# A two-layer hybrid encoder on one core: softmax rows divided after the weighted sum, with the inverse row sums turned on TensorE and spread through DRAM

## The chip, the cores and the metric

The kernel runs on one core of one Trainium2 chip. The metric is the device time of one execution in microseconds (us). Three runs of the kernel before gave a median of 2450.9 us (2449.78 to 2452.65); one further execution was profiled.

## The reference

Two layers, each of them a half-step SwiGLU feed-forward, a mixer with three branches, and a second half-step feed-forward, on 512 tokens of 1024 channels in f32. The change lies in the two attention branches of the mixer, A (chunked, with a learned bias by distance) and C (causal, with cumulative forget gates as bias); each has 8 heads of 64 channels. For one head:

```python
qf = rms_norm(q, gq) * (dh ** -0.5)
kf = rms_norm(k, gk)
logits = einsum('bqhd,bkhd->bhqk', qf, kf) + bias      # masked entries: -1e30
p = softmax(logits, axis=-1)
out = einsum('bhqk,bkhd->bqhd', p, v)
```

The outputs of all heads are concatenated, multiplied by a branch matrix, gated, summed over the branches and multiplied by an output matrix.

## The kernel before

**Arithmetic.** Nearly every product of f32 matrices is made of three TensorE matmuls: each operand is split into a high part (a cast, on ScalarE) and a low part (source minus high part, mostly on VectorE); `triple` (lines 119 to 121) issues high x high, high x low and low x high. `wchunk` loads a 512 KB piece of weights and splits it (cast on line 271, subtraction on line 273). `split_to` does the same for activations (lines 378 and 379).

**Order of the work.** Python code emits the instructions. A counter `pe[0]` adds up nominal TensorE work (one unit is about one 512-column matmul). `later(delay, fn)` puts a step into a list with a due time on that counter, and `poll()`, called before every `triple`, runs what has come due. The tile framework then places each emitted instruction in its engine's queue, and may move it ahead of others. Every engine works through its queue in order.

**Attention.** `attention` goes through the 8 heads, and in a head through 4 blocks of 128 queries (`logits(h, i)`, with (i+1) x 128 keys). Between the blocks a *filler* emits other TensorE work: for branch A the projections of branch C (`fill_a`), for branch C the merge of branch A's output (`fill_c`). One block does this:

1. `logits`: two matmuls into a PSUM tile `mm` (lines 951, 952); VectorE adds the bias, negates and takes the row minimum (line 955, `mx`); ScalarE takes the exponential and, in the same instruction, the row sums `sm` (line 959); VectorE inverts them (`rs`, line 961); the exponentials are multiplied by `rs`, on GpSimd for blocks 0 to 2 and on VectorE for block 3 (line 962).
2. `turn`, 24 units later: TensorE transposes the 128x128 pieces (line 974), ScalarE casts the result (line 978), VectorE subtracts (line 979).
3. `weigh`, 14 units after every second block: TensorE multiplies with the values (lines 996, 997). The two halves of the output stand in two halves of the partitions; ScalarE copies one (line 1000), VectorE adds the other (line 1001), and `split_to` makes the high part on ScalarE and the low part on GpSimd (line 379), 64 partitions by 256 queries each.

Two heads make a *pair* p: their outputs are the lower and the upper 64 partitions of one output tile. PSUM has four tiles `mm` and four tiles `acc`; SBUF has 17 tiles of the tag `b` (4 KB a partition), which hold queries, keys, outputs and weights in turn, two of `t1` and three of `t2`.

**Queries and keys.** `proj_qk` projects, sums squares by head, computes the inverse norms and multiplies the four tiles by them (line 839, two on VectorE and two on GpSimd). Its inner `turn(p)` transposes a pair and writes the scaled result: on ScalarE to a head's own partitions (line 853), and for queries a second time, on ScalarE, to the other 64 partitions (line 856); the low part is made on VectorE (line 859).

**Other GpSimd work at that time.** Memsets for the low parts (line 857), the causal mask added to the bias strips of branch C (`strip_c`, line 937). DMAs are issued by SyncE's queue, except the four per layer that save x to DRAM (line 1119, GpSimd's queue).

Of the kernel before, what the change touches and what calls it, by code (L numbers as in the profile page):

```python
# [15 lines left out]
F32 = mybir.dt.float32  # L16
F32R = mybir.dt.float32r
I32 = mybir.dt.int32
AF = mybir.ActivationFunctionType
ALU = mybir.AluOpType  # L20
AX = mybir.AxisListType

P = 128
T = 512
# [6 lines left out]
HD = 64  # L31
NT = T // P
# [8 lines left out]
def encoder_kernel(tc, xT, c, w_ada, b_ada, gains, w_gate, w_up, w_down, w_qkv, w_f, w_ubg,  # L41
# [22 lines left out]
    def st(shape, dt, tag, bufs):  # L64
        return sb.tile(shape, dt, tag=tag, bufs=bufs, name=nm(tag))
# [4 lines left out]
    def mmt(shape=(P, T)):  # L70
        return ps.tile(list(shape), F32, tag="mm", bufs=4, name=nm("mm"))

    def blk(tag, dt=F32R):
        bufs = {"xv": 4, "v2": 4, "b": NB}[tag]
        return st([P, 2, T], dt, tag, bufs)
# [22 lines left out]
    def later(delay, fn, group=None):  # L98
        t = Task(pe[0] + delay, fn, group)
        tasks.append(t)  # L100
        return t
# [70 lines left out]

    x_dram = dr.tile([4, P, 2 * T], F32, name="x_dram")
    fv_dram = [dr.tile([H, FVLEN], F32, name=f"fv_dram{l}") for l in range(L)]

    last = {}

# [199 lines left out]
    def split_to(hi, lo, src, lo_eng=nc.vector):  # L377
        nc.scalar.copy(hi, src)  # L378
        lo_eng.tensor_tensor(lo, src, hi.bitcast(F32), op=ALU.subtract)  # L379
# [438 lines left out]
    def proj_qk(l, col, gcol, is_q, res, pre=None, norm=None):  # L818
        lows = []
        qs = []  # L820

        def evac(t, a):
            if t == 0:
                qs.extend((st([P, NT, T], F32, "ptb", 2), st([P, NT, H], F32, "qss", 1)))
            qn, ss = qs
            nc.scalar.copy(qn[:, t, :], a)
            sq = t2(T)
            nc.scalar.activation(sq, a, AF.Square)  # L828
            nc.vector.tensor_reduce(ss[:, t, :], sq.rearrange("p (h d) -> p h d", h=H), axis=AX.X, op=ALU.add)

        yield from proj(l, col, evac, pre, norm)
        qn, ss = qs
        v = st([P, NT * H], F32, "nt_v32", 2)
        nc.vector.tensor_scalar(v, ss.rearrange("p t h -> p (t h)"), 1.0 / HD, EPS, op0=ALU.mult, op1=ALU.add)
        r = rsqrt(v, NT * H)
        for t in range(NT):
            q3 = qn[:, t, :].rearrange("p (h d) -> p h d", h=H)
            eng = nc.vector if t % 2 else nc.gpsimd
            eng.tensor_tensor(q3, q3, r[:, t * H:(t + 1) * H].unsqueeze(2).to_broadcast([P, H, HD]), op=ALU.mult)

        def turn(p):
            pt = mmt()
            for t in range(NT):
                nc.tensor.transpose(pt[:, t * P:(t + 1) * P], qn[:, t, p * P:(p + 1) * P], ident)
            pe[0] += 2.2
            b = blk("b")
            if is_q:
                lows.append(blk("b"))
            first, second = slice(0, HD), slice(HD, P)
            for odd, (own, other) in enumerate(((first, second), (second, first))):  # L850
                dst = b[:, odd, :]
                gc = gcol[own, :]
                nc.scalar.activation(dst[own, :], pt[own, :], AF.Identity, scale=gc)
                low = dst[other, :]
                if is_q:
                    nc.scalar.activation(low, pt[own, :], AF.Identity, scale=gc)
                    nc.gpsimd.memset(lows[p][other, odd, :].bitcast(F32), 0.0)
                    low = lows[p][own, odd, :]
                nc.vector.scalar_tensor_tensor(low, pt[own, :], gc, dst[own, :].bitcast(F32),
                                               op0=ALU.mult, op1=ALU.subtract)  # L860
            res.append((b, lows[p]) if is_q else b)

        todo = [lambda p=p: turn(p) for p in range(4)]
        turns.append(todo)

        def ready(p):
            if len(todo) >= 4 - p:
                if heads[0] < (Q_GATE if is_q else K_GATE)[p]:
                    later(8, lambda: ready(p))
                else:  # L870
                    while len(todo) >= 4 - p:
                        todo.pop(0)()

        for p in range(4):
            later(TURN + 12 * p, lambda p=p: ready(p))
# [64 lines left out]
    def attention(qs, ks, vs, strip, ys, filler, budget, group):  # L940


        open_pt = {}

        def logits(h, i, strips):
            p, off = divmod(h, 2)
            (q, ql), k = qs[p], ks[p]
            odd = h % 2
            n = (i + 1) * P
            s = mmt()  # L950
            mm(s[:, :n], q[:, odd, i * P:(i + 1) * P], k[:, odd, :n], start=True, stop=False)
            mm(s[:, :n], ql[:, odd, i * P:(i + 1) * P], k[:, odd, :n], start=False, stop=True)
            lg = t1(T)[:, :n]
            mx = st([P, 1], F32, "mx", 4)
            nc.vector.tensor_tensor_reduce(out=lg, in0=s[:, :n], in1=strips[i], scale=-1.0, scalar=BIG,
                                           op0=ALU.add, op1=ALU.min, accum_out=mx)
            pr = t2(T)[:, :n]
            sm = st([P, 1], F32, "sm", 4)
            nc.scalar.activation(pr, lg, AF.Exp, bias=mx, scale=-1.0, accum_out=sm)
            rs = st([P, 1], F32, "rs", 4)  # L960
            nc.vector.reciprocal(rs, sm)
            (nc.vector if i == NT - 1 else nc.gpsimd).tensor_scalar(pr, pr, rs, None, op0=ALU.mult)
            pe[0] += 0.5 * (i + 1.5)
            later(LAG_T, lambda: turn(h, i, pr), group)

# [18 lines left out]
        def weigh(h, half, pt):  # L984
            p, off = divmod(h, 2)
            rows = slice(off * HD, off * HD + HD)
            other = slice(HD - off * HD, 2 * HD - off * HD)
            if off == 0 and half == 0:
                ys.append(blk("b"))
            y = ys[p]  # L990
            o = mmt((P, HALF))
            nj = 2 * half + 2
            for j in range(nj):
                q0 = P if j == nj - 1 else 0
                v2 = vs[j][:, h, :, :].rearrange("p a d -> p (a d)")
                mm(o[:, q0:], v2, pt[:, 0, j, q0:], start=(j == 0), stop=False)  # L996
                mm(o[:, q0:], v2, pt[:, 1, j, q0:], start=False, stop=(j == nj - 1))  # L997
            cols = slice(half * HALF, (half + 1) * HALF)
            yl = t1(T)[:, :HALF]
            nc.scalar.copy(yl[rows, :], o[other, :])  # L1000
            nc.vector.tensor_tensor(yl[rows, :], o[rows, :], yl[rows, :], op=ALU.add)
            split_to(y[rows, 0, cols], y[rows, 1, cols], yl[rows, :], nc.gpsimd)
            pe[0] += 1.0 * nj

        for h in range(H):
            strips = strip(h)
# [13 lines left out]
            for _ in filler:  # L1020
                pass

    LAG_T, LAG_V = 24, 14


    def pool_front(l, g):
# [244 lines left out]
```

## Time and profile before

| what | before |
|---|---|
| median of three runs | 2450.9 us |
| profiled execution | 2450.88 us |
| its span, first to last instruction | 2448.9 us |
| mean granted TensorE clock | 0.998 |
| instructions | 34028 |

The span leaves 2.0 us of the profiled execution outside. In the profile PE is TensorE's matmuls and PEld its weight loads (each matmul has one, which overlaps the matmul ahead of it), DVE is VectorE, ACT ScalarE, POOL GpSimd, SP SyncE. A name such as L974 is the line of the kernel. "mm<-ident,t" says that an instruction writes a tile `mm` and reads `ident` and a tile of tag `t1` or `t2` (numbers in names are left out). An idle stretch of an engine is put down to the instruction that ended it, its releaser.

### The profile page before, as it was taken

To read this page: it belongs to the slowest core of one execution; us is meant where nothing else is said; L and a number is where in the kernel's file an instruction comes from. 1 tells how busy PE (TensorE), PEld (TensorE's weight loads), DVE (VectorE), ACT (ScalarE), POOL (GpSimd) and SP (SyncE) were. 2 spreads that over 40 slices of the span, in tenths; PEclk is the share of its full clock that TensorE was granted. 3 is DMA by queue.
4 is the path that set the end of the run, shared out by engine and by line. 5 is a ranking of instruction groups with operands and counts; after the bars stand their busy time and mean duration, and the time that the engine had idled before them with its cause. 6 is when DMAs were issued, how large, how long until landed. Compare 5 with 4: busy or idle time off the path is not lost. (4 is left out here: it accounts for less than half of the span.)

```text
span 2448.9 us, 34028 instructions
## 1 busy us (share of the span) xinstructions
PE 2396.8 (98%) x12966; PEld 2051.8 (84%) x12966; DVE 1600.5 (65%) x2859; ACT 1110.3 (45%) x1888; POOL 377.3 (15%) x439
## 2 busy tenths in 40 slices
PE   7999999999999999999999999999999999999999
PEld 5798888777888898988898888878777888988888
DVE  8978766677643378787678656477765434765463
ACT  5333345677642353333453334366765333533341
POOL 3000002144532110000000000123354322000000
PEclk9999999999999999999999999999999999999999
DMA  7756543222323426565327423223133234233232
GB/s 284 251 170 209 198 147 113 78 82 88 116 91 103 142 75 240 174 206 198 129 85 243 138 86 121 103 90 96 61 109 99 95 111 139 87 104 112 67 114 78
DMA packets 116279, 320.23 MB, mean 131 GB/s; under 512 B 11122, under 2 KB 13298, under 8 KB 116116
## 3 DMA queue, kind: packets, MB, share of 16 engines
q1 hardware_dynamic: 114962, 313.86, 38.3%
q0 software_dynamic: 1152, 4.19, 0.4%
q8 instruction: 102, 1.67, 0.3%
q14 instruction: 61, 0.50, 0.1%
q10 hardware_dynamic: 2, 0.00, 0.0%
HBM read 311.64 MB, written 6.38 MB: 130 GB/s over the span
## 5 line engine op out<-in xcount | busy, mean ns | idle before, releaser
L271 ACT CAST whi<-raw 128x1024 fp32r<-128x1024 f32 (+1 forms) x325 | 338.2, 1044 | 595.1 <-PE mm L120 289.2
L273 DVE TENSOR_TENSOR wlo<-raw,whi 128x1024 fp32r<-128x1024 f32 x317 | 392.2, 1240 | 197.4 <-ACT whi L271 194.2
L121 PE MATMUL mm<-hhi,wlo 128*128 128x512 f32 x744 | 289.8, 390 | 0.7 <-DVE wlo L273 0.4
L119 PE MATMUL mm<-hhi,whi 128*128 128x512 f32 x744 | 290.2, 390 | 0.0
L120 PE MATMUL mm<-hlo,whi 128*128 128x512 f32 x744 | 290.0, 390 | 0.0
L119 PE MATMUL acc<-b,whi 128*128 128x512 f32 (+1 forms) x704 | 264.1, 376 | 1.7 <-ACT b L378 1.7
L121 PE MATMUL acc<-b,wlo 128*128 128x512 f32 (+1 forms) x704 | 262.1, 374 | 3.5 <-DVE wlo L273 3.5
L120 PE MATMUL acc<-b,whi 128*128 128x512 f32 (+1 forms) x704 | 262.4, 373 | 0.0
L197 DVE CUSTOM_DVE_ANT_0 v<-v,b,badac 128x1024 f32<-128x1024 f32 x144 | 188.3, 1316 | 60.9 <-DMA v<-in_w_ada_dram 60.7
L119 PE MATMUL acc<-hhi,whi 128*128 128x512 f32 x480 | 190.7, 399 | 1.7 <-ACT hhi L738 1.7
L121 PE MATMUL acc<-hhi,wlo 128*128 128x512 f32 x480 | 188.9, 394 | 0.0
L120 PE MATMUL acc<-hlo,whi 128*128 128x512 f32 x480 | 188.5, 393 | 0.2 <-DVE hlo L741 0.2
L121 PEld LDWEIGHTS mm<-hhi,wlo 128*128 128x128 f32 x744 | 139.7, 188 | 30.9 <-DVE wlo L273 1.6
L119 PEld LDWEIGHTS mm<-hhi,whi 128*128 128x128 f32 x744 | 140.0, 188 | 27.9
L120 PEld LDWEIGHTS mm<-hlo,whi 128*128 128x128 f32 x744 | 139.7, 188 | 27.4
L121 PEld LDWEIGHTS acc<-b,wlo 128*128 128x128 f32 x704 | 133.8, 190 | 27.2 <-DVE wlo L273 4.6
L119 PEld LDWEIGHTS acc<-b,whi 128*128 128x128 f32 x704 | 133.3, 190 | 23.8 <-ACT b L378 2.6
L120 PEld LDWEIGHTS acc<-b,whi 128*128 128x128 f32 x704 | 133.3, 189 | 23.2 <-DVE b L379 0.9
L119 PE MATMUL acc<-whi,hhi 128*128 128x512 f32 x336 | 137.7, 411 | 4.4 <-ACT t L828 3.7
L120 PE MATMUL mm<-b,whi 128*128 128x512 f32 (+1 forms) x384 | 135.8, 354 | 0.0
L119 PE MATMUL mm<-b,whi 128*128 128x512 f32 (+1 forms) x384 | 135.8, 354 | 0.0
L121 PE MATMUL mm<-b,wlo 128*128 128x512 f32 (+1 forms) x384 | 135.6, 354 | 0.0
(300 smaller groups left out, 5598.3 us busy)
## 6 DMA issues: line engine op xcount, KB each, us to landing
v<-in_w_ada_dram SPq DMA_DIRECT2D x144, 512.0 KB, 4.4
raw<-in_w_down_dram SPq DMA_DIRECT2D x88, 512.0 KB, 3.5
raw<-in_w_up_dram SPq DMA_DIRECT2D x82, 512.0 KB, 3.4
b<-in_w_gate_dram SPq DMA_DIRECT2D x76, 512.0 KB, 5.3
raw<-in_w_ubg_dram SPq DMA_DIRECT2D x56, 512.0 KB, 3.3
raw<-in_w_qkv_dram SPq DMA_DIRECT2D x42, 512.0 KB, 3.7
raw<-in_w_branch_dram SPq DMA_DIRECT2D x24, 512.0 KB, 3.6
raw<-in_w_out_dram SPq DMA_DIRECT2D x16, 512.0 KB, 3.3
```

The costliest lines, as they stand in the source:

```text
L119: mm(o, lh, rh, start=start, stop=False, skip_group_check=onto)
L120: mm(o, lh, rl, start=False, stop=False, skip_group_check=onto)
L121: mm(o, ll, rh, start=False, stop=stop, skip_group_check=onto)
L197: dot = nc.vector.tensor_tensor_reduce(out=raw, in0=raw, in1=silc[0], scale=1.0, scalar=badac[:, l, j, d:d + 1], op0=ALU.mult, op1=ALU.add ...
L271: nc.scalar.copy(hi, raw)
L273: lo_eng.tensor_tensor(lo, raw, hi.bitcast(F32), op=ALU.subtract)
```

## The change

In words:

- **The division moves.** The exponentials are transposed and multiplied with the values undivided. The eight row sums of a pair (two heads, four blocks) are collected in the columns of one 128x8 tile. 26 units after the pair's last exponential, `send` inverts it on VectorE, turns it on TensorE into 8x128, copies it out of PSUM on ScalarE and writes it to DRAM (4 KB, GpSimd's queue). 24 units later `spread` reads it back twice (GpSimd's queue), 512 inverse sums broadcast over the 64 partitions of each head. 20 units later `norm_rows` multiplies the pair's whole output by it (VectorE, 128x512) and splits it: cast on ScalarE, subtraction on VectorE.
- `weigh` now leaves its f32 sum in a tile of tag `b` (output and inverse sums of the pair), and no longer splits it.
- **Norms.** All four tiles of line 839 are multiplied on VectorE.
- **Second query copies.** GpSimd copies them from the first ones in SBUF, where ScalarE wrote them from PSUM.

```diff
+    inv_dram = {(g, p): dr.tile([2 * NT, P], F32, name=f"inv_dram_{g}{p}") for g in "ac" for p in range(4)}
...
-            eng = nc.vector if t % 2 else nc.gpsimd
+            eng = nc.vector
...
                 if is_q:
-                    nc.scalar.activation(low, pt[own, :], AF.Identity, scale=gc)
+                    nc.gpsimd.tensor_copy(low, dst[own, :])
...
+        sums, rows_of = {}, {}
...
-            sm = st([P, 1], F32, "sm", 4)
-            nc.scalar.activation(pr, lg, AF.Exp, bias=mx, scale=-1.0, accum_out=sm)
-            rs = st([P, 1], F32, "rs", 4)
-            nc.vector.reciprocal(rs, sm)
-            (nc.vector if i == NT - 1 else nc.gpsimd).tensor_scalar(pr, pr, rs, None, op0=ALU.mult)
+            if odd == 0 and i == 0:
+                sums[p] = st([P, 2 * NT], F32, "sm", 2)
+            nc.scalar.activation(pr, lg, AF.Exp, bias=mx, scale=-1.0,
+                                 accum_out=sums[p][:, odd * NT + i:odd * NT + i + 1])
+            if odd and i == NT - 1:
+                later(LAG_S, lambda: send(p), group)
...
             if off == 0 and half == 0:
-                ys.append(blk("b"))
-            y = ys[p]
+                rows_of[p] = st([P, 2, T], F32, "b", NB)
+            y = rows_of[p][:, 0, :]
...
-            nc.vector.tensor_tensor(yl[rows, :], o[rows, :], yl[rows, :], op=ALU.add)
-            split_to(y[rows, 0, cols], y[rows, 1, cols], yl[rows, :], nc.gpsimd)
+            nc.vector.tensor_tensor(y[rows, cols], o[rows, :], yl[rows, :], op=ALU.add)
             pe[0] += 1.0 * nj
+
+        def send(p):
+            rs = st([P, 2 * NT], F32, "rs", 1)
+            nc.vector.reciprocal(rs, sums[p])
+            tp = mmt()
+            nc.tensor.transpose(tp[:2 * NT, :P], rs, ident)
+            flat = st([2 * NT, P], F32, "flat", 1)
+            nc.scalar.copy(flat, tp[:2 * NT, :P])
+            pe[0] += 0.5
+            nc.gpsimd.dma_start(inv_dram[group, p], flat)
+            later(LAG_R, lambda: spread(p), group)
+
+        def spread(p):
+            for off in range(2):
+                r = inv_dram[group, p].rearrange("(h i) q -> h (i q)", h=2)[off:off + 1, :]
+                nc.gpsimd.dma_start(rows_of[p][off * HD:(off + 1) * HD, 1, :], r.broadcast_to([HD, T]))
+            later(LAG_N, lambda: norm_rows(p), group)
+
+        def norm_rows(p):
+            y = blk("b")
+            ys.append(y)
+            full = rows_of[p][:, 0, :]
+            nc.vector.tensor_tensor(full, full, rows_of[p][:, 1, :], op=ALU.mult)
+            split_to(y[:, 0, :], y[:, 1, :], full)
...
-    LAG_T, LAG_V = 24, 14
+    LAG_T, LAG_V, LAG_S, LAG_R, LAG_N = 24, 14, 26, 24, 20
```

Behind the first added line all line numbers rise, so that line 955 of before is line 957 of the changed kernel, 979 is 982, 1001 is 1004, 273 is 274 and 937 is 938.

The queues show the move at three places, all in branch C of the first layer. VectorE before, for one head (`t` and `lg` are tiles of `t1` and `t2`; `rs` are the inverse sums of one block, `mx` its row minimum):

```order
L961 RECIPROCAL rs_6113<-sm_6111 128x1
L979 TENSOR_TENSOR ptb_6044<-mm_6119,ptb_6044 128x4x128
L955 ISA t_1255_6135,mx_6136<-mm_6132,strip_6051 128x384
L955 ISA mx_6136 128x1
L979 TENSOR_TENSOR pta_6144<-mm_6145,pta_6144 128x128
L961 RECIPROCAL rs_6141<-sm_6139 128x1
L1001 TENSOR_TENSOR t_1263_6164<-mm_6155,t_1263_6164 64x256
L955 ISA t_1266_6180,mx_6181<-mm_6177,ssum_6053 128x512
```

VectorE in the changed kernel, from the inverse sums of a pair (line 1009) on:

```order
L1009 RECIPROCAL rs_5669<-sm_5312 128x8
L274 TENSOR_TENSOR wlo_5793<-raw_5790,whi_5792 128x1024
L1004 TENSOR_TENSOR b_5474<-mm_5630,t_1090_5635 64x256
L957 ISA t_1099_5661,mx_5662<-mm_5658,strip_5610 128x256
L957 ISA mx_5662 128x1
L982 TENSOR_TENSOR ptb_5603<-mm_5676,ptb_5603 128x4x128
```

And seven rows on, around the multiplication of that pair's output (line 1028):

```order
L982 TENSOR_TENSOR pta_5697<-mm_5720,pta_5697 128x2x128
L957 ISA t_1116_5733,mx_5734<-mm_5730,ssum_5612 128x512
L957 ISA mx_5734 128x1
L1028 TENSOR_TENSOR b_5474<-b_5474 128x512
L274 TENSOR_TENSOR wlo_5929<-raw_5926,whi_5928 128x1024
```

The reciprocal that stood behind every block's row minimum is gone; one for eight blocks stands in its place, and 13 rows behind it the multiplication, which waits for both reads of `spread`; behind it stand the next weights' low parts (line 274).

GpSimd before, for about one head (line 962 multiplies a block by its inverse sums, line 379 makes a low part, line 937 adds the mask to a bias strip):

```order
L962 TENSOR_SCALAR t_1146_5755<-t_1146_5755,rs_5758 128x128
L379 TENSOR_TENSOR b_5589<-t_1150_5769,b_5589 64x256
L962 TENSOR_SCALAR t_1161_5800<-t_1161_5800,rs_5803 128x256
L962 TENSOR_SCALAR t_1168_5828<-t_1168_5828,rs_5831 128x384
L379 TENSOR_TENSOR b_5589<-t_1174_5854,b_5589 64x256
L937 TENSOR_TENSOR strip_6051<-strip_6051,cmask 128x128 x3
L937 TENSOR_TENSOR ssum_5900<-ssum_5900,cmask 128x128
```

GpSimd in the changed kernel, for one pair of heads:

```order
L938 TENSOR_TENSOR strip_5766<-strip_5766,cmask 128x128 x3
L938 TENSOR_TENSOR ssum_5612<-ssum_5612,cmask 128x128
L1015 DMA inv_dram_c_127<-flat_5673 8x128
L1021 DMA b_5474<-inv_dram_c_127 64x512 x2
L938 TENSOR_TENSOR strip_5894<-strip_5894,cmask 128x128 x3
L938 TENSOR_TENSOR ssum_5768<-ssum_5768,cmask 128x128
```

The multiplications and low parts have left GpSimd; the write to DRAM and the two reads follow each other directly in its queue, so that GpSimd stands still until the write has landed, with the next heads' masks behind it.

TensorE before, around the transposes of a head's last block (line 974):

```order
L120 MATMUL acc_5790<-hlo,whi_5786 128x512
L974 MATMUL mm_5809<-ident,t_1133_5714 128x128 x4
L121 MATMUL acc_5790<-hhi,wlo_5787 128x512
L951 MATMUL mm_5822<-b_5120,b_4593 128x384
L952 MATMUL mm_5822<-b_5120,b_4594 128x384
```

The same place in the changed kernel, with the turn of the pair's inverse sums (line 1011) ahead of the transposes:

```order
L119 MATMUL acc_5654<-hhi,whi_5650 128x512
L1011 MATMUL mm_5671<-ident,rs_5669 8x128
L977 MATMUL mm_5676<-ident,t_1076_5587 128x128 x4
L120 MATMUL acc_5654<-hlo,whi_5650 128x512
L121 MATMUL acc_5654<-hhi,wlo_5651 128x512
L953 MATMUL mm_5689<-b_5041,b_4554 128x384
L954 MATMUL mm_5689<-b_5041,b_4555 128x384
```

One instruction is added to TensorE's queue, and all behind it wait with it for line 1009. From line 1011 to the multiplication of line 1028 TensorE's queue holds 40 to 45 matmuls for the four pairs of branch A, and 30, 29, 29 and 22 for those of branch C.

## The prediction

> **What bounds the kernel now.** I read the page, then busy time by stage, then what the weight loads wait for, then the rows of the operations that the change touches. The page first:
>
> ```profile
> PE 2396.8 (98%) x12966; PEld 2051.8 (84%) x12966; DVE 1600.5 (65%) x2859; ACT 1110.3 (45%) x1888; POOL 377.3 (15%) x439
> ```
>
> TensorE is the bound; time can come only out of its gaps or its own work. By stage (busy time and count of PE, PEld, DVE, ACT, POOL; then the granted clock, the DMA share and GB/s), the two attention stages and the stretch behind the first:
>
> ```profile
> 425.00:700.00 275.00, 261.70 (x1347) 211.43 (x1346) 188.35 (x461) 184.72 (x397) 108.75 (x143) 0.99 0.29 92
> 1625.00:1900.00 275.00, 260.05 (x1342) 208.78 (x1341) 188.76 (x458) 182.44 (x392) 112.08 (x148) 1.00 0.29 88
> 700.00:875.00 175.00, 175.00 (x835) 147.53 (x834) 70.55 (x79) 59.76 (x81) 44.13 (x35) 1.00 0.35 115
> ```
>
> In the third row PE has no gap; in the first two it lacks 13.3 and 15.0 us. That counts too little, since the record of a matmul covers part of the gap behind it. A weight load is short, so its waits show the gaps whole. What the loads wait for (us in total, times, longest), the lines that occur in attention:
>
> ```profile
> PEld mm L974 <- POOL t L962: 14.0, 20, 1.1
> PEld acc L119 <- ACT t L828: 6.6, 8, 1.7
> PEld mm L951 <- DVE t L1001: 6.5, 6, 1.5
> PEld mm L974 <- issue: 4.6, 8, 0.9
> PEld mm L951 <- DVE ptb L979: 4.2, 4, 1.9
> PEld mm L974 <- DVE ptb L979: 3.9, 5, 1.0
> PEld mm L951 <- DVE mx L955: 3.6, 6, 0.8
> PEld mm L997 <- DVE ptb L979: 3.0, 6, 0.5
> PEld mm L951 <- issue: 2.6, 2, 1.3
> PEld mm L996 <- ACT ptb L978: 2.0, 5, 0.6
> PEld mm L996 <- DVE ptb L979: 1.0, 2, 0.5
> ```
>
> They add up to 52.0 us: 14.0 for GpSimd's multiplication, 22.2 for VectorE (6.5 + 4.2 + 3.9 + 3.6 + 3.0 + 1.0), 8.6 for ScalarE, 7.2 without a releaser. This is all that the change can win, 2.1% of the time.
>
> **The base.** The profiled execution took 2450.88 us (span 2448.9 and 2.0 outside it), the median of the runs is 2450.9; the sum is made against 2450.9.
>
> **The wait for the division: -14.0.** One block, from the exponential's last row to its transposes:
>
> ```profile
> 527.48 0.19 ACT L959 ACTIVATION_READ_ACCUMULATOR t<-t,mx 128x1 f32 x1
> ...
> 528.67 0.60 POOL L962 TENSOR_SCALAR t<-t,rs 128x128 f32<-128x128 f32 x1
> ...
> 529.32 0.14 PEld L974 LDWEIGHTS mm<-ident,t 128*128 128x128 f32 x1 [0.94 <-POOL t L962]
> ```
>
> The exponentials are there at 527.67, the transposes start at 529.32: 1.65 us go to inverting, multiplying and handing over, and this is the smallest block. The longest wait on line 962 is 1.1 us, so with the exponential as releaser all 20 waits end. Next late is the exponential itself; TensorE asked at most 1.1 us before it got the tile, and this one was exponentiated 1.65 us before, so 0.55 us are to spare. Ends 10 and 14; I take 14.
>
> **VectorE's relief: -12.** Prices of what leaves and comes (count, then ns min/median/max), and VectorE's standstill ahead of the reciprocals:
>
> ```profile
> L961 DVE RECIPROCAL rs<-sm x128: 144/162/166, 465.4 to 1887.2; 128x1 f32<-128x1 f32 x128
>   ACT t L959: 37.6, 66
> L962 DVE TENSOR_SCALAR t<-t,rs x32: 465/487/781, 473.4 to 1887.4; 128x512 f32<-128x512 f32 x32
> L839 DVE TENSOR_TENSOR ptb<-ptb,nt_z x16: 691/1528/1533, 417.1 to 1747.1; 128x512 f32<-128x512 f32 x16
> L379 DVE TENSOR_TENSOR ptb<-ssum,ptb x8: 691/691/693, 692.8 to 1922.6; 128x512 fp32r<-128x512 f32 x8
> L962 POOL TENSOR_SCALAR t<-t,rs x96: 602/927/1253, 465.7 to 1882.5; 128x128 f32<-128x128 f32 x32, 128x256 f32<-128x256 f32 x32, 128x384 f32<-128x384 f32 x32
> L379 POOL TENSOR_TENSOR b<-t,b x64: 723/737/1750, 477.6 to 1894.2; 64x256 fp32r<-64x256 f32 x64
> ```
>
> Out: 128 x 0.162 = 20.7 and 32 x 0.487 = 15.6 us of work, and the 37.6 us in which VectorE stood behind an exponential, since a reciprocal was next in its queue. In: 16 pairs x (0.16 + 0.69 + 0.69) = 24.6. The norms' 32 tiles on VectorE alone cost 32 x 0.69 = 22, where 16 cost up to 16 x 1.53 = 24 beside GpSimd's: even. So VectorE gets 20.7 + 15.6 + 37.6 - 24.6 = 49 us of 550 back, and is earlier at lines 955, 979 and 1001, which TensorE waits for. How much of the 22.2 us that ends, no row says: none, where a wait belongs to a chain of PE, ACT and DVE that has nothing queued ahead of it; all, where it is only queueing. VectorE is 68% busy in these stages, and I take half, 11, plus 1 for the `t1` tiles, which were held until GpSimd's line 379 was done. Ends: 0 and 22.
>
> **GpSimd's copies** (32 of 64x512) are within that half. They read SBUF, as the removed operations did:
>
> ```profile
> 417.15 2.14 DVE L839 TENSOR_TENSOR ptb<-ptb,nt_z 128x512 f32<-128x512 f32 x2
> 417.26 2.93 POOL L839 TENSOR_TENSOR ptb<-ptb,nt_z 128x512 f32<-128x512 f32 x2 [17.75 <-DVE nt_z L287]
> 419.21 2.06 DVE L273 TENSOR_TENSOR wlo<-raw,whi 128x1024 fp32r<-128x1024 f32 x1
> ```
>
> ```profile
> L273 DVE TENSOR_TENSOR wlo<-raw,whi 128x1024 fp32r<-128x1024 f32 x317 | 392.2, 1240 | 197.4 <-ACT whi L271 194.2
> ```
>
> Line 273 takes 2.06 us beside GpSimd's line 839, against 1.24 on average. If each copy held up VectorE by that 0.82 us, 26 us of the relief would go. But 96 + 64 + 16 of GpSimd's operations with such reads leave for those 32, so the balance is a gain or nothing. [...]
>
> **ScalarE's relief: -2.** Out go the second query copies and the 64 small casts, in come 16 casts of 128x512 and 16 copies of 8x128, for which the nearest row is the cast of 128x128:
>
> ```profile
> L856 ACT ACTIVATE b<-mm,qg x32: 682/685/688, 425.2 to 1730.4; 64x512 fp32r<-64x512 f32 x32
> L378 ACT CAST b<-t x64: 388/405/411, 477.1 to 1893.8; 64x256 fp32r<-64x256 f32 x64
> L378 ACT CAST ptb<-ssum x8: 620/622/622, 692.1 to 1921.9; 128x512 fp32r<-128x512 f32 x8
> ```
>
> ```profile
> L978 ACT CAST pta<-mm 128x128 fp32r<-128x128 f32 x16 | 4.2, 263 | 2.7 <-PE mm L974 2.7
> ```
>
> 32 x 0.685 + 64 x 0.405 - 16 x (0.62 + 0.26) = 34 us of 367 less. Of the 8.6 us that TensorE waits for ScalarE I take a quarter, since most of it (line 828) stands in the projections; ends 0 and 8.6. The 7.2 us without a releaser I leave.
>
> **TensorE's added work: +2.** Sixteen turns of 8x128, at most as dear as a 128x128 transpose. Four of those follow each other in 0.42 us:
>
> ```profile
> 525.16 0.42 PEld L974 LDWEIGHTS mm<-ident,t 128*128 128x128 f32 x4 [0.65 <-issue]
> ```
>
> 16 x 0.11 = 1.8 us; ends 0 and 2.
>
> **The wait in `send`: +4.** TensorE waits for line 1009, and all matmuls behind it with it. The exponential is 26 units old by then, so only VectorE's queue can make it late; the nearest row is line 951's wait on line 955, at most 0.8 us and 0.6 on average. Ends 0 and 16 x 0.8 = 13; I take 0.25 each, since most of such turns found VectorE in time.
>
> **The way through DRAM: +4.** Line 1028 waits for the landing of `spread`, and VectorE stands with it. Small writes and GpSimd's DMAs:
>
> ```profile
> x_dram<-xv POOLq DMA_DIRECT2D x8, 512.0 KB, 3.2
> out_dram<-xv SPq DMA_DIRECT2D x8, 128.0 KB, 1.7
> L1119 POOL DMA_DIRECT2D x_dram<-xv x8: 573/573/762, 365.9 to 1596.4; - x8
> L271 ACT CAST whi<-raw 128x1024 fp32r<-128x1024 f32 (+1 forms) x325 | 338.2, 1044 | 595.1 <-PE mm L120 289.2
> ```
>
> Write and read land in 1.7 us each at best (the 128 KB row) and 3.2 at worst (512 KB); an issue takes 0.57. The round trip is 0.1 (turn) + 0.3 (copy) + 1.7 + 0.57 (the second read's issue) + 1.7 = 4.4 us at least; with three issues counted, 3.2 twice and 1.0 more for a ScalarE busy with a cast of weights (line 271, below) 9.5 at most; middle 7.0. Against it stands TensorE's work between: 275 / 1347 = 0.204 us a matmul makes 8.2 to 9.2 us in branch A (40 to 45 matmuls), 6.0 in branch C (29 or 30), and 0.7 more for the row minimum of 128x512 that VectorE does last (an estimate, from the subtraction of that size above). The fourth pair of C has 4.5 us only, but behind it come three pool projections of 24 matmuls, at 175 / 835 = 0.21 us each 15 us of work whose weights are split ahead. At 7.0 us each of six pairs of C holds VectorE for 0.3 us, 2 in all, and the flush of A's last pair ahead of the merge about 1 in each layer: 4. Ends 0 and, at 9.5 us, 20 (6 x 2.8 in C, 2 x 0.6 for A's third pairs, 2 for the flushes). [...]
>
> **Sum:** -14 - 12 - 2 + 2 + 4 + 4 = -18, so 2433 us. Its own range, with the relief between a quarter and three quarters: 2425 to 2441.
>
> **Rivals.**
>
> *The relief is total: 2408.* All waits on VectorE and ScalarE end and nothing is lost on the new ones: -14 - 22 - 9 + 2 = -43. For it: 49 us of VectorE's time against 22 us of waits. Against it: the chains keep their length.
>
> *Only the division's wait goes: 2447.* -14 + 2 + 4 + 4 = -4. For it: the other waits come in clusters (6 times up to 1.9 us) at the change of heads, where turns and weighings pile up whatever the load. This is inside 0.2%, about what a measurement of this kernel can tell from no change.
>
> *VectorE is held for the spread rows: 2461, slower.* GpSimd's queue stands until the write has landed, then issues two reads; at 9.5 us VectorE is held 20 us, which uses up its relief and comes back as gaps in PE: -14 - 2 + 2 + 4 + 20 = +10. It decides from 8.0 us a trip, where 10 us are held (6 x 1.3 and 2). Against it: GpSimd's 512 KB writes landed in 3.2 us, as SyncE's do. [...]
>
> That the change doesn't do what it says is left out: the queues show what is removed and added.
>
> **How the numbers follow.** Forecast 0.55, total relief 0.2, only the division 0.15, the held VectorE 0.1. Faster by over 0.2% (below 2446): 0.55 + 0.2 + 0.03 of the third = 0.78; same 0.12; slower 0.1. The range goes from the second case to a little above the third, 2408 to 2452, and leaves the last out.
>
> **What would show it.** Right: no waits of line 977 on anything but line 962's exponential, waits on lines 957, 982 and 1004 about halved, VectorE idle ahead of line 1028 under 0.5 us a time, busy PE in the two stages up by 5 us or more a stage. Wrong: weight loads of line 1011 waiting for line 1009 by over 0.5 us each; VectorE idle for microseconds ahead of line 1028; GpSimd's copies stretching line 274 beyond 1.3 us on average.

## The result and the profile after

| what | before | after |
|---|---|---|
| median of the runs made side by side | 2451.78 us (4 runs, 2449.78 to 2453.22) | 2426.67 us (4 runs, 2424.64 to 2428.91) |
| profiled execution | 2450.88 us | 2428.91 us |
| its span | 2448.9 us | 2427.1 us |
| mean granted TensorE clock | 0.998 | 0.998 |
| instructions | 34028 | 33735 |

The ratio is 0.9899, with a 95% interval of 0.9887 to 0.9911: faster by 25 us, where the forecast was 18. The profiled execution is the slowest of the four. Lines move: the row minimum is line 957, the exponential 962, the transposes 977, their casts and subtractions 981 and 982, the products with the values 999 and 1000, the copy and the sum behind them 1003 and 1004. In the experiments numbers can be off by up to three more.

The page's busy times after the change:

```profile
PE 2389.4 (98%) x12982; PEld 2053.3 (85%) x12982; DVE 1590.1 (66%) x2763; ACT 1074.4 (44%) x1824; POOL 253.0 (10%) x343
```

VectorE's work fell by only 10 us, ScalarE's by 36 (34 were worked out), GpSimd's by 124. The two attention stages by window (the second sits 24 us earlier than before), same columns as before:

```profile
425.00:700.00 275.00, 270.16 (x1410) 221.29 (x1409) 188.18 (x418) 170.06 (x369) 60.04 (x113) 1.00 0.34 103
1601.00:1876.00 275.00, 268.06 (x1397) 219.78 (x1396) 188.29 (x423) 170.23 (x369) 48.14 (x97) 0.99 0.34 103
```

Busy PE rises by 8.5 and 8.0 us a stage, and 63 and 55 more matmuls fit into the same 275 us. What the weight loads still wait for, the lines of the attention stages:

```profile
PEld mm L977 <- ACT t L962: 4.9, 2, 2.9
PEld mm L953 <- issue: 3.6, 6, 0.9
PEld mm L977 <- DVE ptb L982: 3.2, 3, 2.2
PEld mm L1000 <- DVE ptb L982: 2.9, 6, 0.5
...
PEld mm L977 <- DVE b L860: 2.1, 4, 0.6
PEld acc L119 <- ACT t L829: 1.3, 2, 0.7
PEld mm L999 <- DVE b L1004: 1.3, 2, 0.6
PEld mm L953 <- ACT flat L1013: 1.0, 4, 0.3
PEld mm L977 <- DVE mx L957: 0.9, 2, 0.5
...
PEld mm L1011 <- issue: 0.7, 2, 0.3
PEld mm L1011 <- DVE b L860: 0.5, 2, 0.2
```

No row names GpSimd's multiplication any more (14.0 us before). The three longest waits are new, and all stand ahead of transposes: two for an exponential (2.9 and 1.9 us), and one of 2.2 us for a tile that VectorE has still to read. VectorE's groups at the steps that were added or moved (busy time, mean ns; then VectorE's standstill ahead of them):

```profile
L274 DVE TENSOR_TENSOR wlo<-raw,whi 128x1024 fp32r<-128x1024 f32 x317 | 390.4, 1234 | 196.6 <-ACT whi L272 193.5
L840 DVE TENSOR_TENSOR ptb<-ptb,nt_z 128x512 f32<-128x512 f32 x32 | 20.0, 686 | 0.2
L860 DVE SCALAR_TENSOR_TENSOR b<-mm,qg,b 64x512 fp32r<-64x512 f32 x32 | 23.6, 748 | 7.8 <-ACT b L854 7.4
L1028 DVE TENSOR_TENSOR b<-b 128x512 f32<-128x512 f32 x16 | 11.2, 700 | 28.1 <-DMA b<-inv_dram_c 24.0 <-DMA b<-inv_dram_a 4.1
```

The last row is the surprise: VectorE stands 28.1 us for the spread inverse sums, which is more than the 20 us with which the slower rival was priced, and the kernel is faster all the same. One way through DRAM in branch C, from the timeline of the changed kernel (start, duration, engine, and in brackets the idle time ahead):

```profile
596.08 0.25 ACT L1013 COPY flat<-mm 8x128 f32<-8x128 f32 x1
...
596.80 0.52 POOL L1015 DMA_DIRECT2D inv_dram_c<-flat  x1
600.80 1.05 POOL L1021 DMA_DIRECT2D b<-inv_dram_c  x2 [3.48 <-DMA inv_dram_c<-flat]
...
604.69 0.71 DVE L1028 TENSOR_TENSOR b<-b 128x512 f32<-128x512 f32 x1 [2.99 <-DMA b<-inv_dram_c]
```

From the copy to the multiplication it is 8.6 us (7.5 to 10.1 in the ten pairs that held VectorE), of which VectorE stood the last 2.99. The write of 4 KB landed late enough that GpSimd stood 3.48 us for it. Where the standstill reaches TensorE shows at the change from branch A to branch C in the second layer:

```profile
1783.09 0.69 DVE L1028 TENSOR_TENSOR b<-b 128x512 f32<-128x512 f32 x1 [2.55 <-DMA b<-inv_dram_a]
1783.70 0.28 DVE L957 CUSTOM_DVE_ANT_0 t<-mm,strip 128x128 f32<-128x128 f32 x1
...
1784.03 0.40 ACT L962 ACTIVATE t<-t,mx 128x128 f32<-128x128 f32 x1 [3.41 <-DVE mx L957]
...
1784.57 0.18 PEld L977 LDWEIGHTS mm<-ident,t 128*128 128x128 f32 x1 [2.92 <-ACT t L962]
```

Read upwards: the transpose waits 2.92 us for the exponential, the exponential for the row minimum, and the row minimum stands in VectorE's queue behind the held multiplication, with which it has nothing to do.

### The profile page after: what moved, and what is told of

It reads as the page before. It is cut to its first block, busy times and chain, and to the rows that moved or that the text cites. A ratio compares the mean times of both kernels' runs of the same rounds, so it can differ in the third digit from the quotient of the medians.

```text
span 2427.1 us, 33735 instructions
## 1 busy us (share of the span) xinstructions
PE 2389.4 (98%) x12982; PEld 2053.3 (85%) x12982; DVE 1590.1 (66%) x2763; ACT 1074.4 (44%) x1824; POOL 253.0 (10%) x343
## 5 line engine op out<-in xcount | busy, mean ns | idle before, releaser
L274 DVE TENSOR_TENSOR wlo<-raw,whi 128x1024 fp32r<-128x1024 f32 x317 | 390.4, 1234 | 196.6 <-ACT whi L272 193.5
```

What stands on the lines that cost most here:

```text
L274: lo_eng.tensor_tensor(lo, raw, hi.bitcast(F32), op=ALU.subtract)
```

## The experiments

All were timed in five rounds beside the kernel before. A ratio is the time over that of the kernel before, with its 95% interval. The expectations name their theories anew in each set and say what each claims.

A yardstick that grew out of the runs: all waits of the weight loads in 415 to 700 us and 1600 to 1900 us of each trace, added up by the engine that is named as the releaser (us):

| kernel | GpSimd | VectorE | ScalarE | no releaser | sum | time (us) |
|---|---|---|---|---|---|---|
| before | 14.4 | 25.1 | 8.8 | 8.7 | 57.0 | 2450 to 2452 |
| after | 0 | 13.9 | 8.6 | 6.7 | 29.8 | 2426.67 |
| only the division | 0 | 17.5 | 13.6 | 5.5 | 38.6 | 2432.82 |
| only the norms | 15.7 | 20.7 | 9.0 | 8.2 | 53.6 | 2451.7 |
| only the copies | 9.1 | 23.4 | 4.6 | 4.2 | 41.9 | 2439.8 |
| after, with unused reciprocals | 0 | 10.4 | 7.1 | 8.2 | 25.7 | 2422.57 |
| after, with a multiplication by one | 14.3 | 18.7 | 3.1 | 6.3 | 42.4 | 2440.26 |
| after, multiplication due later | 0 | 9.8 | 8.1 | 6.0 | 24.4 | 2422.69 |
| after, two more transfers | 0 | 18.0 | 17.3 | 12.2 | 48.2 | 2456.18 |
| after, row minima first | 0 | 9.1 | 4.4 | 9.5 | 23.4 | 2419.34 |
| before, query copies emitted later | 10.8 | 22.6 | 7.7 | 9.0 | 51.1 | 2449.75 |
| before, multiplication on VectorE | 0 | 28.5 | 11.0 | 14.3 | 53.8 | 2449.89 |
| before, query copies on both | 14.1 | 25.2 | 9.0 | 8.5 | 56.8 | 2451.98 |
| row minima first, longer distances | 1.1 | 12.8 | 6.6 | 3.9 | 25.4 | 2426.99 |

What stands for TensorE itself as releaser, 2 us at most, is in the sum alone. The sum follows the time roughly; two kernels are clearly slower than their sums: the one with two more transfers and the one with longer distances. It is of one execution each (for only the division the slowest of five, 2437.75 us), and leaves out what is lost outside the two stretches: the first save of x to DRAM, ahead of which no edit changes anything, comes at 362.6 to 366.0 us in the traces.

**Which of the three parts it is.** First only the division, the other two parts undone:

```diff
-            eng = nc.vector
+            eng = nc.vector if t % 2 else nc.gpsimd
...
-                    nc.gpsimd.tensor_copy(low, dst[own, :])
+                    nc.scalar.activation(low, pt[own, :], AF.Identity, scale=gc)
```

> The changed kernel with the norms' tiles split between VectorE and GpSimd as before, and the second query copies on ScalarE as before: the move of the division alone. Theory 1 (the division's move is the whole gain: it takes the reciprocals and GpSimd's multiplications out of the chain): 2427 us, within 3 of the changed kernel. Theory 2 (a good part comes from the two rebalancings, since TensorE's waits for ScalarE fell from 8.6 to about 2 us): 2433 us or more.

Measured: 2432.82 us, ratio 0.9925 (0.9912 to 0.9939), -18 us of the 25. This lies between the two theories, almost at the second: the division is most of the gain and not the whole. Next, on the kernel before, only the norms:

```diff
-            eng = nc.vector if t % 2 else nc.gpsimd
+            eng = nc.vector
```

> The kernel before with all four norm tiles of a projection on VectorE. Theory 1: no difference, 2451 us within 2 (32 tiles of 0.69 us take the place of 16 of up to 1.53). [...]

Measured: 2451.7 us, ratio 1.0006 (0.9998 to 1.0015): nothing, as the price of 22 against up to 24 us had it. VectorE's tiles of line 839 are shorter with GpSimd's gone from beside them (686 ns in the mean, 1216 before), but twice as many. And only the copies:

```diff
-                    nc.scalar.activation(low, pt[own, :], AF.Identity, scale=gc)
+                    nc.gpsimd.tensor_copy(low, dst[own, :])
```

> The kernel before with the second query copies on GpSimd. Theory 1: no difference or a small loss, 2451 to 2454 us, since GpSimd has the multiplications in its queue as well. Theory 2 (ScalarE's 22 us of relief matter): 2447 us or less.

Measured: 2439.8 us, ratio 0.9952 (0.994 to 0.9965). Theory 2 holds, by more than its bound: the smallest part of the change is worth about 11 us alone, and 6 on top of the division (2432.82 to 2426.67). In its weight loads:

```profile
PEld mm L974 <- POOL t L962: 8.7, 13, 1.0
...
PEld acc L119 <- ACT t L828: 2.5, 4, 0.7
```

14.0 and 6.6 us before. A wait that is booked on GpSimd's multiplication fell by 5 us although GpSimd got 20 us more to do: the chain ahead of it (exponential, copies out of PSUM) runs on ScalarE. It fell where the copies of branch C's queries stand (500 to 590 us and 1710 to 1800 us: from 10.4 to 4.8 us), and nowhere else (3.6 to 4.0). That both parts shorten the same chain would explain why 18 and 11 make 25.

**Is it VectorE's relief?** The prediction booked 12 us for VectorE's time, most of it the standstill behind exponentials. So the reciprocals were put back into the changed kernel, with results that nobody reads:

```diff
+            again = st([P, 1], F32, "again", 4)
+            nc.vector.reciprocal(again, sums[p][:, odd * NT + i:odd * NT + i + 1])
```

> The changed kernel with a reciprocal of each block's row sums put back behind its exponential, as before; its result is used by nothing. Theory A (VectorE's standstill behind the exponentials delayed the rest of its queue, and ending that is a good part of the gain): VectorE stands about 35 us ahead of these reciprocals again and the time rises by 6 to 12 us, to 2433 to 2439. Theory B (the queue didn't matter, only the chain from exponential to transpose): at most 2 us more, 2429 or less.

```profile
L965 DVE RECIPROCAL again<-sm 128x1 f32<-128x1 f32 x128 | 20.2, 159 | 31.3 <-ACT t L962 30.6
```

VectorE works 20.2 us more and again stands 31.3 us behind exponentials, and the time is 2422.57 us, ratio 0.9889 (0.9876 to 0.9902), no slower than the changed kernel, as theory B had it. (By the ratios the two cannot be told apart, since their intervals overlap. The test is not quite clean: the standstill for the spread rows falls with it, from 28.1 to 22.1 us. Against the version below in which that standstill is halved, this one is 3 us slower.) The relief as the prediction reasoned it falls.

**Is it the length of the chain?** The multiplication was put back between exponential and transposes, by ones and without a reciprocal, on the engines of before:

```diff
+            (nc.vector if i == NT - 1 else nc.gpsimd).tensor_scalar(pr, pr, ones[:, 0:1], None, op0=ALU.mult)
```

> The changed kernel with the multiplication put back into the chain, blocks 0 to 2 on GpSimd and block 3 on VectorE as before, by a column of ones, so without any reciprocal. If the chain through GpSimd is worth the 14 us that the trace of before shows for it: 2437 to 2443 us, with weight loads waiting 9 to 14 us for GpSimd again. If the chain was slack and only the reciprocals' standstill mattered: 2430 us or less.

```profile
PEld mm L978 <- POOL t L964: 14.3, 16, 2.6
PEld mm L953 <- DVE b L1005: 4.8, 6, 1.5
```

The wait on GpSimd is back at 14.3 us (14.0 before), and the time at 2440.26 us, ratio 0.9965 (0.9953 to 0.9976): 13.6 us lost by the medians, 16 by the ratios. The same link can be tried without DRAM: on the kernel before, VectorE multiplies all four blocks.

```diff
-            (nc.vector if i == NT - 1 else nc.gpsimd).tensor_scalar(pr, pr, rs, None, op0=ALU.mult)
+            nc.vector.tensor_scalar(pr, pr, rs, None, op0=ALU.mult)
```

> The kernel before, in which VectorE multiplies all four row blocks by the inverse row sums (before: the last block on VectorE, three on GpSimd). Nothing goes through DRAM and the copies stay as before. It puts about 26 us of work on VectorE (96 multiplications of 128 to 384 columns) and takes GpSimd out of the chain between the exponentials and the transposes. Theory 1 (what the wait for the division costs is GpSimd's slow multiplication and the hand-over to it, 14.0 us of waits): about half of it goes, since the chain keeps the reciprocal and a shorter multiplication: 2440 to 2446 us, a ratio near 0.997. Rival (VectorE's load is what counts): the multiplications queue behind its other work, and the weight loads of the transposes wait for VectorE in place of GpSimd: 2449 to 2462 us.

```profile
PEld mm L974 <- issue: 8.5, 11, 2.4
PEld mm L951 <- DVE mx L955: 5.7, 6, 1.7
...
PEld mm L974 <- DVE t L962: 2.1, 5, 0.6
```

Measured: 2449.89 us, ratio 0.9998 (0.9989 to 1.0006). VectorE's multiplication takes 403 ns in the mean of all four blocks, where GpSimd's took 927 in that of the three shorter ones: the faster engine brings nothing. The waits on the multiplication fall from 14.0 to 2.1 us, but line 974 waits 8.5 us without a visible releaser (4.6 before) and the row minima are later, 5.7 us (3.6). So the link has to leave the chain, as in the change; a quicker link in a busier queue only moves the waits. Together with the unused reciprocals this suggests which VectorE time counts here: not the engine's total, but work that stands ahead of something the transposes need.

**What the copies' gain is.** On the kernel before, ScalarE's second copies were emitted behind both halves' first copies and low parts, so that VectorE's low part (line 859) need not stand behind them:

```diff
-                    nc.scalar.activation(low, pt[own, :], AF.Identity, scale=gc)
...
+            for odd, (own, other) in halves:
+                if is_q:
+                    nc.scalar.activation(b[:, odd, :][other, :], b[:, odd, :][own, :].bitcast(F32), AF.Copy)
```

> The kernel before, in which ScalarE still makes the second query copies, but each of them is emitted behind both halves' first copies and low parts (it reads the first copy from SBUF), so that VectorE's low part has no second copy ahead of it to stand behind. ScalarE's work stays the same, 32 copies of about 0.69 us. Theory 1 (the gain of GpSimd's copies, 0.48% on the kernel before, is VectorE's standstill behind the second copy, 20.3 us): that standstill falls to about 9 us, as with GpSimd's copies, and the time to 2437 to 2444 us, a ratio of about 0.996. Theory 2 (it is the 22 us of ScalarE's work that leave): the standstill falls, but the time stays within 0.15% of before, 2447 to 2453 us, and weight loads wait for the low part as long as before.

Line 859 of the kernel before, and of this one:

```profile
L859 DVE SCALAR_TENSOR_TENSOR b<-mm,qg,b 64x512 fp32r<-64x512 f32 x32 | 24.0, 750 | 20.6 <-ACT b L856 20.3
```

```profile
L859 DVE SCALAR_TENSOR_TENSOR b<-mm,qg,b 64x512 fp32r<-64x512 f32 x32 | 23.8, 749 | 13.5 <-ACT b L854 13.3
```

Measured: 2449.75 us, ratio 0.9996 (0.9988 to 1.0005). The standstill fell by 7 of the 11 us by which GpSimd's copies lower it, and brought nothing. The other side: GpSimd makes the copy that is used, and ScalarE still makes its own, where nobody reads it.

```diff
+                    nc.scalar.activation(lows[p][other, odd, :], pt[own, :], AF.Identity, scale=gc)
```

> The kernel before with GpSimd's second query copies (which took 11 us off it), and ScalarE's 32 second copies left in at their old place as well, written where nobody reads them (GpSimd's clearing of the same half follows). So ScalarE's work and order are those of before, while GpSimd makes the copy that is used. Theory 2 (the copies' gain is the 22 us of ScalarE's work that leave, since the version with the copies moved behind the low parts gained nothing): the gain is gone, 2447 to 2452 us, and the weight loads' waits behind the projections' squares and the second copies are back near 6.6 us. Theory 1 (the gain comes from what stands behind the copy that is used: VectorE's low part and the tile): most of it stays, 2438 to 2444 us, as long as VectorE's standstill ahead of the low part stays near 9 us; if that goes back to 20 us, this run does not tell the two apart.

Measured: 2451.98 us, ratio 1.001 (1.0001 to 1.0019). The gain is gone. But VectorE's standstill is back too, since the unused copy goes into the tile that the low part is written to:

```profile
L860 DVE SCALAR_TENSOR_TENSOR b<-mm,qg,b 64x512 fp32r<-64x512 f32 x32 | 24.0, 750 | 20.9 <-ACT b L857 20.7
```

So this run alone does not tell load from standstill, as its expectation allowed for. Taken with the run before it, ScalarE's 22 us of work is the likelier cause: less standstill at equal load gained nothing, and every run that took the copies off ScalarE gained. Load without the standstill was not run; that much stays open.

**What the standstill for the spread rows costs.** First two more transfers on the way, a second write and a read back:

```diff
+            nc.gpsimd.dma_start(inv2_dram[group, p], flat)
+            nc.gpsimd.dma_start(flat, inv2_dram[group, p])
```

> The changed kernel with two more transfers in each pair's way: the inverse sums go to DRAM, back and to DRAM again before the spread, some 8 us longer. Theory 1 (VectorE's standstill ahead of the pair's multiplication is free): it grows from 28 us to 50 or more, and TensorE shows new waits only ahead of the merge of branch A, at most 8 us in all: 2435 us or less. Rival (a held microsecond of VectorE costs about one of TensorE): 2450 us or more.

```profile
L1031 DVE TENSOR_TENSOR b<-b 128x512 f32<-128x512 f32 x16 | 11.3, 704 | 49.1 <-DMA b<-inv_dram_c 28.8 <-DMA b<-inv_dram_a 20.3
```

```profile
PEld mm L954 <- issue: 10.3, 8, 4.5
PEld mm L1000 <- ACT ptb L982: 9.0, 10, 1.6
PEld mm L846 <- DVE ptb L983: 6.1, 2, 3.6
```

Measured: 2456.18 us, ratio 1.0024 (1.0012 to 1.0035): slower than before the change. In branch C the standstill hardly grows (24.0 to 28.8 us), in branch A it goes from 4.1 to 20.3. In the first layer three held multiplications of branch A (4.23, 4.83 and 3.59 us) are each followed within some 2 us by the end of a long wait of TensorE (3.56, 4.48 and 3.16 us). The granted clock from 425 to 700 us is 0.97, where the changed kernel has 1.00, which by 275 x 0.03 is an estimated 8 us of TensorE's time that the sum of the waits does not hold. So the slower rival exists; the kernel as changed is one longer trip away from it. Then the other direction, a later due time for the multiplication:

```diff
-    LAG_T, LAG_V, LAG_S, LAG_R, LAG_N = 24, 14, 26, 24, 20
+    LAG_T, LAG_V, LAG_S, LAG_R, LAG_N = 24, 14, 26, 24, 44
```

> The changed kernel with the multiplication of the pair's output emitted 44 units behind the reads instead of 20. In the changed kernel's trace VectorE stands 28 us in all ahead of that multiplication. Theory 1 (that standstill is free, since nothing behind it in VectorE's queue is asked for by TensorE in time): VectorE's standstill falls below 10 us and the time stays at 2427 within 3. Rival (a held microsecond of VectorE costs about a microsecond of TensorE): 2410 us or less.

Measured: 2422.69 us, ratio 0.9884 (0.9871 to 0.9898). The test missed its aim: the framework left the multiplication about where it was in VectorE's queue, and the standstill only fell from 28.1 to 24.9 us, so neither theory was tested (the intervals of this ratio and the changed kernel's overlap). The next one ties it down: the multiplication is placed behind the row minimum that was emitted last.

```diff
+            last["mx"] = nc.vector.tensor_tensor_reduce(out=lg, in0=s[:, :n], in1=strips[i], scale=-1.0, scalar=BIG,
+                                           op0=ALU.add, op1=ALU.min, accum_out=mx).ins
...
-            nc.vector.tensor_tensor(full, full, rows_of[p][:, 1, :], op=ALU.mult)
+            with after("mx"):
+                nc.vector.tensor_tensor(full, full, rows_of[p][:, 1, :], op=ALU.mult)
```

> The changed kernel with the pair's multiplication kept behind the row minimum that was emitted last before it, which moves it some 20 matmuls later in VectorE's queue for branch C (an emission 24 units later had left it at the same place). Theory 1 (the standstill is free): VectorE stands below 8 us ahead of it instead of 28, and the time stays at 2427 within 3. Rival: 2410 us or less.

Its multiplication in VectorE's groups, and two rows of its weight loads' waits:

```profile
L1029 DVE TENSOR_TENSOR b<-b 128x512 f32<-128x512 f32 x16 | 11.4, 710 | 13.1 <-DMA b<-inv_dram_c 10.4 <-DMA b<-inv_dram_a 2.7
```

```profile
PEld mm L999 <- issue: 3.3, 2, 1.7
...
PEld mm L977 <- ACT t L962: 0.7, 4, 0.2
```

Measured: 2419.34 us, ratio 0.9876 (0.9863 to 0.9888): faster than both kernels, than the changed one by 7.3 us in the medians and by 5.6 by the ratios (the two were timed beside different runs of before). Neither theory holds: the standstill is halved, not below 8 us, and 15 us less of it bring 6 to 7 us, so a held microsecond was neither free nor worth a whole one of TensorE. The two late exponentials are gone (4.9 to 0.7 us), and so are the waits of the transposes on line 982 (3.2 us). Of those, 3.0 us stood behind holds of branch C; this is the longer one, in the changed kernel's second layer:

```profile
1804.71 0.85 DVE L1028 TENSOR_TENSOR b<-b 128x512 f32<-128x512 f32 x1 [4.44 <-DMA b<-inv_dram_c]
1805.48 1.21 DVE L274 TENSOR_TENSOR wlo<-raw,whi 128x1024 fp32r<-128x1024 f32 x1
1806.62 0.55 DVE L982 TENSOR_TENSOR ptb<-mm,ptb 128x384 fp32r<-128x384 f32 x1
...
1807.21 0.42 PEld L977 LDWEIGHTS mm<-ident,t 128*128 128x128 f32 x4 [2.17 <-DVE ptb L982]
```

Line 982, which reads a PSUM tile that the next transposes need, stands behind the held multiplication and a subtraction of weights. Another part is TensorE's clock around the second late exponential, first the changed kernel and then this one:

```profile
1775.00:1800.00 25.00, 22.09 (x124) 17.78 (x123) 16.15 (x43) 14.62 (x42) 6.01 (x12) 0.93 0.44 118
```

```profile
1775.00:1800.00 25.00, 23.40 (x132) 18.89 (x131) 17.51 (x46) 16.49 (x43) 7.82 (x14) 1.00 0.45 141
```

A mean granted clock of 0.93 over 25 us is 25 x 0.07 = 1.75 us of TensorE's time, an estimate; a 128x512 matmul takes 0.63 us in the slow part of that stretch (1785 to 1787 us) and 0.39 or 0.40 ahead of it (1780 to 1782 us). With 4.2 and 3.2 us of waits that end, and 3.0 us of a wait that grows (line 999, without a releaser, 0.3 us before), that makes 6 us.

**Can the chain be given more room?** The same version with transposes and turns due four matmuls later:

```diff
-    LAG_T, LAG_V, LAG_S, LAG_R, LAG_N = 24, 14, 26, 24, 20
+    LAG_T, LAG_V, LAG_S, LAG_R, LAG_N = 28, 14, 30, 24, 20
```

> The version with the row minima kept ahead of the spread multiplication (2419.3 us), with the transposes of the weights taken 28 instead of 24 matmuls behind their logits and the turn of the sums 30 instead of 26. Theory 1 (no transposes wait for an exponential any more, 0.7 us in all): no gain to be had, 2417 to 2422 us. Rival (the waits that are left, on VectorE's copies of the transposed weights and on the row minima, come from too short a distance): some of about 10 us of them go, 2411 to 2416 us. Against both: more tiles are open at a time, so the logits may wait for a free tile, 2423 us or more.

```profile
PEld mm L977 <- ACT t L962: 4.0, 4, 2.5
...
PEld mm L999 <- DVE pta L982: 3.3, 2, 1.6
```

Measured: 2426.99 us, ratio 0.9905 (0.989 to 0.992), slower than the 0.9876 that it starts from. Waits on the exponential come back (0.7 to 4.0 us), against both theories. The time is where the third expectation had it, but its wait for a free tile is 1.0 us in all and no cause for 7.7. The sum of the waits is only 2 us above that of the version it starts from. By the saves of x to DRAM the loss of 7.7 us between the two traces lies in three places: 2.5 us ahead of the first layer's save, where the edit changes nothing, 2.7 us between the two layers' saves and 2.5 us behind the second's. Its cause stays open.

## Why the prediction was right, and where it was not

The forecast was 2433 us, the time is 2426.67, inside the range and on the right side. By its steps:

- **Division, -14.0: right, in mechanism and size.** All waits on GpSimd's multiplication end, and putting the multiplication back costs 13.6 us (16 by the ratios). The slack of 0.55 us ahead of the transposes held, except at two places between the branches, where another cause made exponentials late. The sign that the transposes would wait for nothing but exponentials did not come: they still wait 3.2 us for line 982 and 2.1 us for line 860, both on VectorE.
- **VectorE's relief, -12: the size came out by luck, its reason did not.** Waits on VectorE in the two stretches fell from 25.1 to 13.9 us, about half as taken. But the step from 49 us that VectorE gets back to its being earlier at the lines that TensorE waits for failed: with 51 us of it taken away again by unused reciprocals, nothing was lost. The 37.6 us behind exponentials were time in which VectorE had nothing urgent queued. That these waits fell is shown; why they did is only partly shown: the chain is a link shorter, and with the multiplication back they were at 18.7.
- **ScalarE's relief, -2: mis-sized.** The copies are worth about 11 us alone and 6 on top of the division. The step that failed is to take only a quarter, "since most of it (line 828) stands in the projections": that wait fell from 6.6 to 1.3 us, and ScalarE's 22 us were, by where GpSimd's wait fell with the copies alone, also in the chain that was booked under GpSimd. A wait is put down to the last link, and a term per engine counts the links before it at nothing.
- **TensorE's turns, +2, and the wait in `send`, +4: too much.** Line 1011 waits 0.7 + 0.5 us in all, and the loads behind line 1013 1.0.
- **The way through DRAM, +4: too cheap, and wrong in both factors.** The trip takes 8.6 us from the copy on in the pair shown, where 7.0 was taken for the whole of it, and VectorE stands 28.1 us where 4 was expected; "VectorE idle ahead of line 1028 under 0.5 us a time" failed, 10 times 2.8 us. Taking half of the standstill away gains 6 to 7 us, so the cost is about that at least.
- **The rival with the held VectorE** had the standstill about right (20 us, against 28.1) and its price wrong: one us of TensorE for each us held. Of branch C's 24.0 us TensorE shows 3.0, the waits of 2.17 and 0.84 us on line 982. At the ends of branch A, where the next row minima stood behind, 4.1 us held cost 4.9. With 49.1 us held it came true.
- **The norms: even,** as worked out. **GpSimd's copies** do not show in VectorE's mean: line 274 takes 1234 ns, 1240 before. One of line 274, at 505.03 us, takes 1.60 us beside a copy; a few of the copies are longer too:

```profile
L857 POOL CAST b<-b x32: 604/610/1342, 424.0 to 1714.4; 64x512 fp32r<-64x512 f32 x32
```

The longest, beside that line 274, takes 1342 ns in place of 610. So at that place both are longer, but the 26 us that 0.82 us a copy would have come to did not come about.

By terms of what was measured: -13.6 for the chain, -6 to -11 for the copies, some -12 on waits for VectorE with an overlap among the three, +6 to +7 for the standstill, nothing for norms and about 2 for turns and `send`. The forecast fell 7 us short of the 25, chiefly since ScalarE's term was too small and those for `send` and the turns were too large; the way through DRAM, taken too cheap, hid some of that.

## What to carry to other kernels

Price a stall by what stands behind it in the engine's queue, not by its length: 31 us behind exponentials cost nothing that could be measured, 2.55 us ahead of the next head's row minimum cost 2.9 us of TensorE and some of its clock (0.93 over 25 us). When an operation sits between a producer and the engine that bounds the kernel, take it out of that chain rather than putting it on a faster engine, and look at every engine along the chain, since the profile books the whole wait on the last one (the wait on GpSimd fell by 5 us when ScalarE lost work). After such a change look where its late inputs land in the queue, and pin that place.

## What the runs showed of the hardware

A small transfer through DRAM was mostly as slow as a large one. GpSimd's write of 4 KB and its reads that spread 2 KB over 64 partitions, from issue to landing in the changed kernel, first the write and then the read:

```profile
DMA to landing us min/median/max: 1.5/3.3/4.4
```

```profile
DMA to landing us min/median/max: 2.7/3.0/6.4
```

The medians, 3.3 and 3.0 us, are near that of GpSimd's 512 KB writes (3.2 us), and not near that of the 128 KB writes by SyncE (1.7 us) from which the lower end was built. Only branch A's writes of 4 KB are near it, with a median of 1.6 us, against 3.4 in branch C. The reads have a tail to 6.4 us.

TensorE's granted clock fell to 0.57 or 0.61 for some 4 us behind some waits, and the length of a single wait did not decide it. Behind the wait of 2.92 us in the changed kernel it is 0.57 from 1784 to 1788 us; in the version with the row minima first, which has no such wait, it is 1.00 from 1775 to 1800 us. In the kernel before it is 0.57 from 597 to 601 us, behind two waits of 0.78 and 0.79 us within 2 us of each other; at the same place of the second layer, with 1.22 and 0.80 us, it stays at 1.00. A wait of 2.50 us is followed by 0.61 in the version with longer distances (582 to 586 us), and by 1.00 in the one with two more transfers (1719 to 1725 us). Why equal waits end differently, and why waits of under 1 us were enough once, the runs do not show.
